# Dilated attention in a two-layer fp32 trunk: value products of two groups made wide, attention steps put in six places of a quarter, one group's scores in plain fp32

## The chip, the cores and the metric

The kernel runs on one core of one Trainium2 chip. The metric is the time of one execution on the device in microseconds, as the median of several runs. In the profile, PE is TensorE's matmul, PEld its weight load, DVE is VectorE, ACT is ScalarE, POOL is GpSimd and SP the engine that issues the loads. L12 is line 12 of the kernel's file.

## The reference

A trunk of two layers works on 256 tokens of width 1024, all in float32. Each layer is: half a SwiGLU feed-forward, a token mixer, half a second SwiGLU feed-forward, each behind an RMS norm and added to the residual. Layer 0 mixes with dilated window attention, layer 1 with latent attention. The change is in layer 0's mixer:

```python
A_PATTERNS = ((128, 1), (512, 4), (2048, 16))     # three groups of 16 heads of width 64
q, k, v = jnp.split(x @ w_in, 3, axis=-1)
q = rope(rmsnorm(q.reshape(shp), q_gain), pos)
k = rope(rmsnorm(k.reshape(shp), k_gain), pos)
for g, (window, dilation) in enumerate(A_PATTERNS):
    o, lse = _dilated_band(q[:, :, sl], k[:, :, sl], v[:, :, sl], window, dilation)
wts = jax.nn.softmax(jnp.stack(lses, axis=0), axis=0)
o = jnp.einsum('gbsh,gbshd->bshd', wts, jnp.stack(outs, axis=0))
return o.reshape(B, S, A_HEADS * A_HEAD_DIM) @ w_out
```

A token of group g attends to earlier tokens at distances that are multiples of the group's dilation, inside its window. The three groups' outputs of a head are merged with weights from their softmax denominators, which is the same as one softmax over the scores of all three groups.

## The kernel before

Every product of weights is taken in three terms: both sides are split into a high part, rounded to the reduced type fp32r, and a low part, and high x high, high x low and low x high are summed in PSUM. `piece` (L86 to L103) does it for the weights: SP loads 1 MB, ACT casts the high part (L101) and DVE subtracts it (L102), in four cuts in this layer. The normed activations stand transposed and split in `xh` and `xl`. Tokens are stored by their residue modulo 4, so that group 1 sees four blocks of 64 tokens, and group 2 sees them through a window that is shifted by 64 tokens.

The dilated layer goes through four quarters of four heads each (`hq`), and through the three groups in a quarter, which makes twelve units. A unit has:

- `qk_products`: q and k of four heads, 512 columns, for two token tiles; two weight pieces (halves of the model width), each 24 products of 512 columns (L483 to L485), with a `filler` between the halves. `norm_rope_a` (L654 to L674) then norms and rotates both token tiles on ACT, DVE and POOL.
- `v_products`: values of the four heads, 256 columns; one piece, 48 products of 256 columns (L499 to L501), then ACT's scaled copies into `v0` (group 0, L506) or `vc` (groups 1 and 2, L509, L512).
- a turn (`turn`, L520): eight PE transposes of the normed q and k; for group 0 ACT and DVE split the result into high and low parts (L526, L527), for the others ACT copies it (L529).

When a quarter's three units are done, its attention follows in six steps during the next quarter. Four of them take scores (`scores(i)`, two heads by one token tile): three fp32r terms for group 0 (L543, 256 keys), small fp32 products of 64x64 for groups 1 and 2 (L550), then the softmax on DVE and ACT (L394 to L401). One step later come the transposes of the weights p (L408, copied by ACT, L410), one more step later the products with the values (L574, L585). Step i thus holds scores(i), the transposes of i-1 and the outputs of i-2, in this order. The two heads of a step stand in rows 0 to 63 and 64 to 127 of PE.

`fill()` sets where this goes: it is called three times a unit (between the halves, behind the norm, behind the values), takes a turn if one waits, else the next attention step. So a quarter has nine places: three turns and six steps. The instructions of an engine run in one order, which a scheduler makes from the program's; it moves an instruction past others where it thinks that its inputs or its buffer are late. PSUM has four banks `acc` for the dense products, three banks `wk` for scores and all transposes, which are used in turn and come free when ACT or DVE has read them, and one bank `ob` for the outputs.

The last quarter's attention is put between parts of the output projection (`out_part`, 24 products of 256 columns for each pair of heads).

## Time and profile before

| | |
|---|---|
| time, median of 3 runs | 1155.69 us (1155.37 to 1155.75) |
| the profiled execution, its own time | 1156.32 us |
| its span | 1154.5 us |
| granted TensorE clock | 0.998 |
| dilated layer in it | 195.7 to 479.2 us, 283.5 us |
| PE busy in that stretch | 282.7 us |
| DVE, ACT busy in it | 224.9 us, 173.8 us |
| HBM read | 194.01 MB, 169 GB/s over the span |

The profile's page has the busy time of every engine, the chain of work that ended last, and groups of instructions. A row of the time line is start, length, engine, line, operation, out<-in and count; the length of a matmul there is its way through the array and overlaps with the next one's. A row of the chain of waits is start, length and what the chain ran through; its lengths do not overlap. An fp32 product is two records in the trace, an fp32r product and a transpose are one.

### The profile page before, as it was taken

The page shows a single profiled execution, that of the slowest core. Times are in us where ns is not written, and L with a number is a line of the kernel's source. Part 1 is how long each engine was busy: PE and PEld are TensorE (multiplying, and loading weights), DVE is VectorE, ACT ScalarE, POOL GpSimd, SP SyncE. Part 2 cuts the span into 40 slices and gives each one's busy share as a digit, 9 for nine tenths or more (in the row PEclk, how much of TensorE's full clock was granted, in tenths as well). Part 3 has the DMA queues.
Part 4 walks back from the last instruction along what each step waited for, and adds up shares of the span by engine and source line. Part 5 has one row for each costly group of instructions (what it writes and reads, how often), then busy time and mean ns, then how long its engine had stood idle before and what let it go on. Part 6 is the DMA issues. An engine that isn't in the chain of part 4 may idle for free.

```text
span 1154.5 us, 19404 instructions
## 1 busy us (share of the span) xinstructions
PE 1140.5 (99%) x7836; PEld 1026.4 (89%) x7836; DVE 836.8 (72%) x1469; ACT 642.8 (56%) x1090; POOL 106.1 (9%) x99
## 2 busy tenths in 40 slices
PE   9999999999999999999999999999999899999998
PEld 8999999888888888889999989999998788999997
DVE  6966667979788767776666796666687897666665
ACT  7544446566656565654544464444576776545442
POOL 2000002212112111200000020000023202000000
PEclk9999999999999999999999999999999999999999
DMA  8655554554443444255555545555532334555540
GB/s 324 233 200 182 183 186 143 219 183 147 146 151 142 145 148 147 93 200 183 192 194 196 180 173 196 183 183 188 193 110 104 110 127 177 181 191 195 189 146 37
DMA packets 29033, 196.30 MB, mean 170 GB/s; under 512 B 3344, under 2 KB 3856, under 8 KB 5904
## 3 DMA queue, kind: packets, MB, share of 16 engines
q1 hardware_dynamic: 28656, 194.55, 47.9%
q8 instruction: 61, 1.00, 0.4%
q10 hardware_dynamic: 288, 0.52, 0.2%
q14 instruction: 28, 0.23, 0.1%
HBM read 194.01 MB, written 1.05 MB: 169 GB/s over the span
## 4 chain that ended last, share of the span: by engine, by line
PE 92%; DVE 5%; ACT 2%; POOL 1%; issue 1%; DMA 0%; SPq 0%; DVEq 0%; POOLq 0%; ACTq 0%
PE up L210 27%; PE up L214 14%; PE acc L112 9%; PE acc L113 9%; PE acc L114 9%; PE acc L483 4%; PE acc L485 3%; PE acc L484 3%; PE acc L499 2%; PE acc L501 2%; PE acc L500 2%; DVE lo L102 2%; PE wk L408 2%; DVE xs L128 1%; PE wk L520 1%; PE ob L574 1%
## 5 line engine op out<-in xcount | busy, mean ns | idle before, releaser
L102 DVE TENSOR_TENSOR lo<-raw,hi 128x512 fp32r<-128x512 f32 (+2 forms) x408 | 448.5, 1124 | 231.8 <-ACT hi L101 231.4
L101 ACT CAST hi<-raw 128x512 fp32r<-128x512 f32 (+2 forms) x408 | 375.7, 964 | 215.8 <-issue 109.9
L210 PE MATMUL up<-xs,hi 128*128 128x512 f32 x1408 | 483.4, 396 | 1.2 <-ACT hi L101 0.7
L214 PE MATMUL up<-xs,lo 128*128 128x256 f32 x1408 | 366.0, 280 | 0.0
L210 PEld LDWEIGHTS up<-xs,hi 128*128 128x128 f32 x1408 | 252.4, 188 | 45.8 <-DVE xs L128 1.3
L214 PEld LDWEIGHTS up<-xs,lo 128*128 128x128 f32 x1408 | 266.3, 189 | 16.6 <-DVE lo L102 0.7
L113 PE MATMUL acc<-hl,hi 128*128 128x256 f32 x704 | 198.0, 282 | 0.2
L114 PE MATMUL acc<-hh,lo 128*128 128x256 f32 x704 | 197.6, 282 | 0.0
L112 PE MATMUL acc<-hh,hi 128*128 128x256 f32 x704 | 195.9, 281 | 0.2 <-ACT hh L237 0.2
L113 PEld LDWEIGHTS acc<-hl,hi 128*128 128x128 f32 x704 | 132.5, 188 | 1.1 <-DVE hl L238 1.0
L112 PEld LDWEIGHTS acc<-hh,hi 128*128 128x128 f32 x704 | 131.7, 188 | 1.8 <-ACT hh L237 0.6
L114 PEld LDWEIGHTS acc<-hh,lo 128*128 128x128 f32 x704 | 132.5, 188 | 0.0
L237 ACT CAST hh<-h 128x256 fp32r<-128x256 f32 x88 | 35.6, 406 | 142.8 <-DVE h L234 142.8
L483 PE MATMUL acc<-hi,xs 128*128 128x512 f32 x192 | 76.6, 399 | 0.0
L485 PE MATMUL acc<-hi,xs 128*128 128x512 f32 x192 | 75.2, 392 | 0.0
L484 PE MATMUL acc<-lo,xs 128*128 128x512 f32 x192 | 74.9, 390 | 0.0
L226 DVE TENSOR_TENSOR gu<-up,rest 128x512 f32<-128x512 f32 x88 | 60.1, 683 | 2.6 <-ACT rest L224 2.4
L230 DVE TENSOR_TENSOR gu<-gu,bc 128x512 f32<-128x512 f32 x88 | 60.2, 687 | 1.4
L143 POOL TENSOR_TENSOR ssq<-sq 128x256 f32<-128x256 f32 x6 | 4.9, 813 | 587.9 <-ACT sq L140 415.2
L659 POOL TENSOR_TENSOR rr<-r,mhalf 128x8 f32<-128x8 f32 x24 | 39.2, 1636 | 196.5 <-DVE r L657 196.5
L499 PE MATMUL acc<-hi,xs 128*128 128x256 f32 x192 | 55.3, 288 | 0.0
L501 PE MATMUL acc<-hi,xs 128*128 128x256 f32 x192 | 54.6, 284 | 0.0
(198 smaller groups left out, 1493.4 us busy)
## 6 DMA issues: line engine op xcount, KB each, us to landing
raw<-in_up SPq DMA_DIRECT2D x87, 1024.0 KB, 4.8
raw<-in_down SPq DMA_DIRECT2D x44, 1024.0 KB, 4.8
raw<-in_a_qk SPq DMA_DIRECT2D x24, 1024.0 KB, 4.8
raw<-in_a_v SPq DMA_DIRECT2D x12, 1024.0 KB, 4.8
raw<-in_a_out SPq DMA_DIRECT2D x4, 1024.0 KB, 4.7
raw<-in_b_out SPq DMA_DIRECT2D x4, 1024.0 KB, 5.0
raw<-in_b_in SPq DMA_DIRECT2D x3, 1024.0 KB, 4.8
raw<-in_b_q SPq DMA_DIRECT2D x4, 576.0 KB, 4.0
```

Of the source, the lines that this page charges most:

```text
L101: self.pin(pinned, nc.scalar.copy(hi[:, c], raw[:, c]))
L102: self.pin(pinned, nc.vector.tensor_tensor(lo[:, c], raw[:, c], hi.bitcast(F32)[:, c], op=ALU.subtract))
L112: self.nc.tensor.matmul(out, wh, xh, start=start and i == 0, stop=False, **kw)
L113: self.nc.tensor.matmul(out, wh, xl, start=False, stop=False, **kw)
L114: self.nc.tensor.matmul(out, wl, xh, start=False, stop=stop and i == n - 1, **kw)
L210: nc.tensor.matmul(ps[:, u].rearrange("p t s -> p (t s)"), hv[:, k, u, :], both, start=k == 0, stop=False, skip_group_check=True)
L214: nc.tensor.matmul(ps[:, u, 0, :], lv[:, k, u, :], xh[:, k, :], start=False, stop=k == KT - 1, skip_group_check=True)
L483: nc.tensor.matmul(pss[tt], xh, hi[:, k, :], start=kk == 0, stop=False)
L484: nc.tensor.matmul(pss[tt], xh, lo[:, k, :], start=False, stop=False)
L485: nc.tensor.matmul(pss[tt], xl, hi[:, k, :], start=False, stop=kk == KT - 1)
L499: nc.tensor.matmul(o, xh, hi[:, k, :], start=k == 0, stop=False)
L501: nc.tensor.matmul(o, xl, hi[:, k, :], start=False, stop=k == KT - 1)
```

## The change

Values of groups 0 and 1 are taken together: `v_near` runs two pieces like `qk_products`, two token tiles of 512 columns (24 products a half), and `v_far` takes group 2 alone, now with ACT's copies behind each of its two token windows instead of behind both. The weights are laid out to match; the number of pieces and of bytes is unchanged. Group 0's turned q and k are kept as plain fp32, and its scores are one fp32 product a head (now L536) in place of three terms. A step does its transposes first, then its outputs, then its scores. The places of a quarter are written out: the middle of q/k unit 0 (third turn and step 5 of the quarter before), behind the wide values (first turn, step 0), the middle of unit 1 (step 1), behind it (step 2), behind the far values (step 3), the middle of unit 2 (step 4, second turn). In the changed file L510 to L512 are all dense products (before L483 to L485 and L499 to L501), L543 are the small scores products (before L550), L567 and L578 the outputs (before L574 and L585); L520 and L408 keep their numbers.

```diff
-            def fill():
-                if turns:
-                    turns.pop(0)()
-                elif todo:
-                    todo.pop(0)()
-
...
+            low, up = slice(0, H), slice(H, P)
+
+            def v_near(hq, v0, vc, filler):
+
+                pss = [self.acc.tile([P, 512], F32, name="acc") for _ in range(NTT)]
+                for h in range(2):
+                    wp = [t.rearrange("p (k c) -> p k c", k=4) for t in self.piece(v_w[3 * hq + h], 4)]
+                    for tt in range(NTT):
+                        token_product(pss[tt], slice(tt * P, (tt + 1) * P), wp, 4 * h, 4)
+                    if h == 0:
+                        filler()
+                for tt in range(NTT):
+                    rs = self.rstd[:, tt : tt + 1]
+                    nc.scalar.activation(v0[:, tt, :], pss[tt][:, :S], AF.Copy, scale=rs)
+                    for a, rows in enumerate((low, up)):
+                        nc.scalar.activation(vc[rows, tt * 2 + a, :], pss[tt][rows, S:], AF.Copy, scale=rs[rows])
+
+            def v_far(hq, vc):
+
+                wp = [t.rearrange("p (k c) -> p k c", k=KT) for t in self.piece(v_w[3 * hq + 2], 4)]
                 ps = self.acc.tile([P, 512], F32, name="acc")
-                for tt in range(NTT):
-                    o = ps[:, tt * S : (tt + 1) * S]
-                    for k in range(KT):
-                        first = tt * P + (H if g == 2 else 0)
-                        xh, xl = (t[:, k, first : first + P] for t in (self.xh, self.xl))
-                        nc.tensor.matmul(o, xh, hi[:, k, :], start=k == 0, stop=False)
-                        nc.tensor.matmul(o, xh, lo[:, k, :], start=False, stop=False)
-                        nc.tensor.matmul(o, xl, hi[:, k, :], start=False, stop=k == KT - 1)
-                low, up = slice(0, H), slice(H, P)
-                for tt in range(NTT):
-                    o = ps[:, tt * S : (tt + 1) * S]
-                    if g == 0:
-                        nc.scalar.activation(v0[:, tt, :], o, AF.Copy, scale=self.rstd[:, tt : tt + 1])
-                    elif g == 1:
-                        for a, rows in enumerate((low, up)):
-                            nc.scalar.activation(vc[rows, tt * 2 + a, :], o[rows], AF.Copy, scale=self.rstd[rows, tt : tt + 1])
-                    else:
-                        for c, rows in ((tt * 2 + 1, low), ((1 - tt) * 2, up)):
-                            nc.scalar.activation(vc[rows, c, :], o[rows], AF.Copy, scale=rw[rows, tt : tt + 1])
+                for w in range(NTT):
+                    o = ps[:, w * S : (w + 1) * S]
+                    token_product(o, slice(w * P + H, (w + 1) * P + H), wp, 0, KT)
+                    for c, rows in ((w * 2 + 1, low), ((1 - w) * 2, up)):
+                        nc.scalar.activation(vc[rows, c, :], o[rows], AF.Copy, scale=rw[rows, w : w + 1])
+
+            def token_product(out, ts, wp, first, n):
+
+                hi, lo = wp
+                for k in range(n):
+                    kk = first + k
+                    xh, xl = self.xh[:, kk, ts], self.xl[:, kk, ts]
+                    nc.tensor.matmul(out, xh, hi[:, k, :], start=kk == 0, stop=False)
+                    nc.tensor.matmul(out, xh, lo[:, k, :], start=False, stop=False)
+                    nc.tensor.matmul(out, xl, hi[:, k, :], start=False, stop=kk == KT - 1)
 
...
-                    if isinstance(dst, tuple):
-                        hi, lo = dst
-                        nc.scalar.copy(hi, tpv)
-                        nc.vector.tensor_tensor(lo, tpv, hi.bitcast(F32), op=ALU.subtract)
-                    else:
-                        nc.scalar.copy(dst, tpv)
+                    nc.scalar.copy(dst, tpv)
 
...
-                    (qh, ql), (kh, kl) = qt[0], kt[0]
-                    for t, (a, b) in enumerate(((qh, kh), (qh, kl), (ql, kh))):
-                        for r in range(2):
-                            nc.tensor.matmul(ss[r][:, :S], a[rs[r], j, ts], b[rs[r], j, :], start=t == 0, stop=t == 2)
+                    for r in range(2):
+                        nc.tensor.matmul(ss[r][:, :S], qt[0][rs[r], j, ts], kt[0][rs[r], j, :], start=True, stop=True)
...
                 def step(i):
                     def go():
-                        if i < 4:
-                            scores(i)
                         if 0 <= i - 1 < 4:
                             turned(i - 1)
                         if 0 <= i - 2 < 4:
                             outputs(i - 2)
+                        if i < 4:
+                            scores(i)
 
                     return go
 
                 return [step(i) for i in range(6)]
 
+
+            steps, late = [lambda: None] * 6, []
             for hq in range(4):
-
-                qt, kt = (
-                    [tuple(at.tile([P, 2, S], F32R, name=n + x, bufs=2) for x in "hl")]
-                    + [at.tile([P, 2, S], F32, name=n, bufs=4) for _ in range(GA - 1)]
-                    for n in ("qt", "kt")
-                )
+                qt, kt = ([at.tile([P, 2, S], F32, name=n, bufs=6) for _ in range(GA)] for n in ("qt", "kt"))
                 v0 = at.tile([P, NTT, S], F32, name="v0", bufs=2)
                 vc = at.tile([P, 2 * NTT, S], F32, name="vc", bufs=2)
-                for g in range(GA):
-                    u = hq * GA + g
-                    if u < 4 * GA - 1:
-                        pss = qk_products(u, fill)
-                        if u == 0:
-                            self.stats()
-                            window_stats()
-                            nc.vector.tensor_scalar(ee, self.var, EPS, None, op0=ALU.mult)
-                        qkn = [self.norm_rope_a(at, pss[tt], tt, ee) for tt in range(NTT)]
-                        fill()
-                        v_products(u, g, v0, vc)
-                        fill()
-                    else:
-                        v_products(u, g, v0, vc)
-                        fill()
-                        pss = qk_products(u, fill)
-                        qkn = [self.norm_rope_a(at, pss[tt], tt, ee) for tt in range(NTT)]
-                        while todo:
-                            fill()
-                    turns.append(lambda qkn=qkn, d=(qt[g], kt[g]): turn(qkn, d))
-                todo.extend(attention(hq, qt, kt, v0, vc))
+
+                def qk(g, *midway):
+                    pss = qk_products(hq * GA + g, lambda: [f() for f in midway])
+                    if hq == 0 and g == 0:
+                        self.stats()
+                        window_stats()
+                        nc.vector.tensor_scalar(ee, self.var, EPS, None, op0=ALU.mult)
+                    qkn = [self.norm_rope_a(at, pss[tt], tt, ee) for tt in range(NTT)]
+                    return lambda d=(qt[g], kt[g]): turn(qkn, d)
+
+                turn0 = qk(0, *late)
+                v_near(hq, v0, vc, lambda: None)
+                turn0()
+                steps[0]()
+                turn1 = qk(1, steps[1])
+                steps[2]()
+                v_far(hq, vc)
+                steps[3]()
+                turn2 = qk(2, steps[4], turn1)
+                late = [turn2, steps[5]]
+                steps = attention(hq, qt, kt, v0, vc)
             out_part(0)
             out_part(1)
-            fill()
+            for f in late:
+                f()
             for k in range(2, KT - 2):
-                fill()
+                steps[k - 2]()
                 out_part(k, range(4 if k == KT - 3 else KT))
-            while todo:
-                fill()
+            steps[4]()
+            steps[5]()
             ks = range(KT - 3, KT)
             self.closing([(0, ks[1:]), (2, ks[1:]), (4, ks), (6, ks)], out_part, accs, finish, 1.0)
```

How the instructions stand on PE is shown at four places of the second quarter. First, where the first scores of a quarter stand. Before, in a place of their own between a unit's q/k and value products (kth, ktl, qth, qtl are the split parts of group 0):

```order
L485 MATMUL acc<-hi,xs 128x512
L543 MATMUL wk<-kth,qth 128x256 x2
L543 MATMUL wk<-ktl,qth 128x256 x2
L543 MATMUL wk<-kth,qtl 128x256 x2
L550 MATMUL wk<-kt,qt 64x64 x8
L499 MATMUL acc<-hi,xs 128x256
```

In the change, behind the last two of the first turn's eight transposes:

```order
L520 MATMUL wk<-ident,t_2660 128x128
L520 MATMUL wk<-ident,t_2674 128x128
L536 MATMUL wk<-kt,qt 128x256
L543 MATMUL wk<-kt,qt 64x64 x4
L510 MATMUL acc<-hi,xs 128x512
L536 MATMUL wk<-kt,qt 128x256
L543 MATMUL wk<-kt,qt 64x64 x4
L511 MATMUL acc<-lo,xs 128x512
```

The two heads, which stood together (x2), now stand apart, with one dense product between them.

Second, the step that ends the scores of a quarter, behind the last value products. Before:

```order
L501 MATMUL acc<-hi,xs 128x256
L543 MATMUL wk<-kth,qth 128x256 x2
L543 MATMUL wk<-ktl,qth 128x256 x2
L543 MATMUL wk<-kth,qtl 128x256 x2
L550 MATMUL wk<-kt,qt 64x64 x8
L408 MATMUL wk<-ident,p 128x128 x3
L574 MATMUL ob<-pt,v_2070 64x128 x3
L408 MATMUL wk<-ident,p 128x128 x3
L574 MATMUL ob<-pt,v_2070 64x128
L585 MATMUL ob<-pt,vc 64x64 x4
```

In the change:

```order
L512 MATMUL acc<-hi,xs 128x256
L408 MATMUL wk<-ident,p 128x128 x6
L536 MATMUL wk<-kt,qt 128x256
L543 MATMUL wk<-kt,qt 64x64 x2
L536 MATMUL wk<-kt,qt 128x256
L543 MATMUL wk<-kt,qt 64x64 x6
L512 MATMUL acc<-hi,xs 128x512
```

The six transposes are together; the outputs of this step have moved ahead, into the far values; and the second head's product stands behind two of the first head's small ones.

Third, where those outputs went, between the two token windows of the far values:

```order
L512 MATMUL acc<-hi,xs 128x256
L567 MATMUL ob<-pt,v_2068 64x128 x4
L578 MATMUL ob<-pt,vc 64x64 x4
L510 MATMUL acc<-hi,xs 128x512
L511 MATMUL acc<-lo,xs 128x512
L510 MATMUL acc<-hi,xs 128x256
```

The second window's first product (the last row) waits for ACT, which copies the first window's values out of the same bank; two products of the next unit stand ahead of it.

Fourth, the third turn and step 5, in the middle of the next quarter's first unit (t_3221 and t_3235 are the two token tiles). Before, turn and outputs had a place each, uncut; in the change:

```order
L512 MATMUL acc<-hi,xs 128x512
L520 MATMUL wk<-ident,t_3221 128x128 x2
L567 MATMUL ob<-pt,v_2068 64x128 x3
L520 MATMUL wk<-ident,t_3235 128x128
L520 MATMUL wk<-ident,t_3221 128x128
L520 MATMUL wk<-ident,t_3235 128x128 x2
L520 MATMUL wk<-ident,t_3221 128x128
L520 MATMUL wk<-ident,t_3235 128x128
L567 MATMUL ob<-pt,v_2068 64x128
L578 MATMUL ob<-pt,vc 64x64 x4
L510 MATMUL acc<-hi,xs 128x512
```

The outputs are split around six of the eight transposes. Other places hold their step in one piece: the second step is six transposes and the scores of both heads, the third six transposes, outputs and scores, the fifth six transposes, outputs and the second turn's eight transposes. Outside the dilated layer the order of every engine is as before.

More of the change, by code (lines that the diff above doesn't have):

```diff
@@ L452, in dilated @@
             out_part, accs = self.out_product(w_out, oth, otl)
-            todo, turns = [], []
             for t in (self.xh, self.xl):
@@ L476, in qk_products @@
                 for h in range(2):
-                    hi, lo = (t.rearrange("p (k c) -> p k c", k=4) for t in self.piece(qk_w[u, h], 4))
+                    wp = [t.rearrange("p (k c) -> p k c", k=4) for t in self.piece(qk_w[u, h], 4)]
                     for tt in range(NTT):
-                        for k in range(4):
-                            kk = h * 4 + k
-                            ts = slice(tt * P, (tt + 1) * P)
-                            xh, xl = self.xh[:, kk, ts], self.xl[:, kk, ts]
-                            nc.tensor.matmul(pss[tt], xh, hi[:, k, :], start=kk == 0, stop=False)
-                            nc.tensor.matmul(pss[tt], xh, lo[:, k, :], start=False, stop=False)
-                            nc.tensor.matmul(pss[tt], xl, hi[:, k, :], start=False, stop=kk == KT - 1)
+                        token_product(pss[tt], slice(tt * P, (tt + 1) * P), wp, 4 * h, 4)
                     if h == 0:
@@ new lines, in dilated @@
+            low, up = slice(0, H), slice(H, P)
[4 more added lines that the diff above has]
+                    for tt in range(NTT):
+                        token_product(pss[tt], slice(tt * P, (tt + 1) * P), wp, 4 * h, 4)
+                    if h == 0:
[5 more added lines that the diff above has]
+                        nc.scalar.activation(vc[rows, tt * 2 + a, :], pss[tt][rows, S:], AF.Copy, scale=rs[rows])
@@ L1024, in _layout @@
     a["a_qk"] = c(qk.reshape(4 * GA, 2, P, PIECE))
-    a["a_v"] = c(w[:, :, 2].transpose(3, 2, 1, 0, 4).reshape(4 * GA, P, PIECE))
+    v = w[:, :, 2].transpose(3, 1, 0, 2, 4)
+    near = v[:, :, :, :2].reshape(4, P, 2, PIECE).transpose(0, 2, 1, 3)
+    a["a_v"] = c(np.concatenate([near, v[:, None, :, :, 2].reshape(4, 1, P, PIECE)], axis=1).reshape(4 * GA, P, PIECE))
     a["a_out"] = c(i["a_w_out"][0].reshape(4, 2, P, D).transpose(0, 2, 1, 3).reshape(4, P, PIECE))
```

2 lines of the change are left out of this document (removed).

## The prediction

> **What bounds the kernel now.** I read the page's busy times and its chain of waits first, then the table of stretches for the dilated layer (195.7 to 479.2 us) and for two of its quarters, cut at the first scores product of a quarter.
>
> ```profile
> PE 1140.5 (99%) x7836; PEld 1026.4 (89%) x7836; DVE 836.8 (72%) x1469; ACT 642.8 (56%) x1090; POOL 106.1 (9%) x99
> PE 92%; DVE 5%; ACT 2%; POOL 1%; issue 1%; DMA 0%; SPq 0%; DVEq 0%; POOLq 0%; ACTq 0%
> ```
> ```profile
> 195.70:479.20 283.50, 282.70 (x2157) 246.10 (x2156) 224.94 (x489) 173.84 (x368) 47.81 (x34) 1.00 0.43 149
> 261.40:325.90 64.50, 64.50 (x491) 55.32 (x490) 51.48 (x115) 40.66 (x85) 9.81 (x7) 1.00 0.44 149
> 325.90:390.50 64.60, 64.60 (x491) 55.39 (x490) 51.58 (x115) 39.37 (x84) 9.86 (x7) 1.00 0.42 147
> ```
> The columns are length, then busy time of PE, PEld, DVE, ACT and POOL, the granted clock, the DMA share and GB/s. In a quarter PE is busy for all of its 64.5 us at full clock, DVE for 51.5 and ACT for 40.7. No wait is left to be taken away: a quarter gets shorter only if PE gets less to do, and any wait that comes new is paid in full. So I price PE's own work, by the distance between starts, since a busy time includes each product's way through the array.
>
> **The dense products.** From the chain of waits inside one stretch:
>
> ```profile
> 216.13 0.23 PE acc L484
> ...
> 219.76 0.23 PE acc L485
> ...
> 226.32 0.12 PE acc L499
> ...
> 232.07 0.23 PE acc L483
> ```
> Sixteen wide (512) products lie between the first two rows: 3.63/16 = 0.227 us. Forty-eight narrow (256) ones lie between the last two: 5.75/48 = 0.120 us. The change replaces eight blocks of 48 narrow products by four of 48 wide ones: 384 x 0.120 = 46.0 us become 192 x 0.227 = 43.5 us. That is **-2.5 us**, the one sure gain. The skill prices this otherwise: the Trainium skill, "TensorEngine Tiling (Array Packing)", section Instruction Overhead, gives each matmul about 60 cycles, which at the 2.4 GHz of its first page would make 192 fewer products worth an estimated 4.8 us; the two paces above allow 2 x 0.120 - 0.227 = 0.013 us a product, and I go by them.
>
> **The places between them.** I price a place as the distance from the last dense product before it to the second one after it, less two dense paces. A turn, a scores step, and a step of six transposes and outputs (PE's time line):
>
> ```profile
> 219.60 0.39 PE L485 MATMUL acc<-hi,xs 128*128 128x512 f32 x1
> 219.83 1.04 PE L520 MATMUL wk<-ident,t 128*128 128x128 f32 x8
> ...
> 220.93 0.40 PE L484 MATMUL acc<-lo,xs 128*128 128x512 f32 x1
> ```
> ```profile
> 325.56 0.39 PE L485 MATMUL acc<-hi,xs 128*128 128x512 f32 x1
> 325.88 0.39 PE L543 MATMUL wk<-kth,qth 64*128 64x256 f32 x2
> 326.11 0.28 PE L543 MATMUL wk<-ktl,qth 64*128 64x256 f32 x2
> 326.22 0.28 PE L543 MATMUL wk<-kth,qtl 64*128 64x256 f32 x2
> 326.43 0.46 PE L550 MATMUL wk<-kt,qt 64*64 64x64 f32 x16
> ...
> 327.05 0.28 PE L500 MATMUL acc<-lo,xs 128*128 128x256 f32 x1
> ```
> ```profile
> 305.34 0.39 PE L485 MATMUL acc<-hi,xs 128*128 128x512 f32 x1
> 305.57 0.82 PE L408 MATMUL wk<-ident,p 128*128 128x128 f32 x6
> 306.32 0.66 PE L574 MATMUL ob<-pt,v 128*64 128x128 f32 x8
> ...
> 307.36 0.28 PE L500 MATMUL acc<-lo,xs 128*128 128x256 f32 x1
> ```
> Turn: 1.33 - 0.45 = 0.88 us. Scores: 1.49 - 0.35 = 1.14. Transposes and outputs: 2.02 - 0.35 = 1.67, of which the six transposes are 0.65 and the outputs 1.02. Uncut, a quarter would need 3 x 0.88 + 4 x 1.14 + 4 x 1.67 = 13.9 us. A quarter of 64.55 us (the mean of the two) with 144 wide products (32.7) and 144 narrow ones (17.25) leaves 14.6. So cutting costs **0.73 us a quarter today**, most of it in the fourth step:
>
> ```profile
> 290.36 0.28 PE L501 MATMUL acc<-hi,xs 128*128 128x256 f32 x1
> ...
> 291.51 0.55 PE L408 MATMUL wk<-ident,p 128*128 128x128 f32 x3
> 291.98 0.65 PE L574 MATMUL ob<-pt,v 128*64 128x128 f32 x6
> 292.56 0.55 PE L408 MATMUL wk<-ident,p 128*128 128x128 f32 x3
> ...
> 293.97 0.39 PE L484 MATMUL acc<-lo,xs 128*128 128x512 f32 x1
> ```
> This place costs 3.61 - 0.35 = 3.26 where 1.14 + 1.67 = 2.81 would do. It also shows the price of a change of tile shape: a transpose takes 0.11 us (0.88 for the turn's eight), so three need 0.33, and 0.47 pass before the outputs start. I take 0.14 for each change.
>
> **Scores in fp32.** Each fp32 product is two records in the trace:
>
> ```profile
> 939.39 0.43 PE wk L825 x2
> ```
> So 256 columns need 2 x 0.217 = 0.43 us. Today the three term rows stand as x2: the two heads (rows 0-63 and 64-127) run side by side, three passes of 0.12, with the first stretched to 0.23. If the fp32 heads pair in the same way, two passes of 0.22 replace 0.46 us and the step stays at **1.14**. Bounds: 1.0 if the step from the 64x128 to the 64x64 shape is free once both are fp32, and 1.57 if the heads run one after the other. I take 1.14, since the pairing is in today's rows. The Trainium skill, "TensorEngine Tiling (Array Packing)", section Key Properties, says that a change of tiling mode drains the engine; by it the lower bound falls away, by the bound alone the sum would be 2.7 us less.
>
> **The new order, place by place.** By the words of the change the steps stay whole; the instruction order above shows that the scheduler still cuts three of a quarter's six places.
> *Turn and first scores:* head 0 alone, one wide product, head 1 alone. The trace has one such cut, in the last quarter:
>
> ```profile
> 448.69 0.28 PE L114 MATMUL acc<-oth,lo 128*128 128x256 f32 x1
> 448.81 1.03 PE L520 MATMUL wk<-ident,t 128*128 128x128 f32 x8
> 449.77 0.38 PE L543 MATMUL wk<-kth,qth 64*128 64x256 f32 x1
> ...
> 450.79 0.27 PE L113 MATMUL acc<-otl,hi 128*128 128x256 f32 x1
> ...
> 452.15 0.28 PE L112 MATMUL acc<-oth,hi 128*128 128x256 f32 x1
> ```
> 2.10 + 1.36 - 4 x 0.12 = 2.98 where 0.88 + 1.14 = 2.02 would do: +0.96. A lone head needs 0.43 now and 3 x 0.12 = 0.36 then, so **+1.1**.
> *Fourth step:* the second head's product stands behind two of the first head's small ones: 0.43 more, one pair of small passes alone (0.11), three more changes of shape (0.42): **+0.96**.
> *Last step, mixed with the third turn:* two more changes of shape and one output product without its partner (0.21): **+0.5**.
> *Second step:* the scores come straight behind the transposes and need the bank of the first three. PE and ACT rows of the last step show when it is free:
>
> ```profile
> 469.65 0.82 PE L408 MATMUL wk<-ident,p 128*128 128x128 f32 x6
> ```
> ```profile
> 470.23 0.86 ACT L410 COPY pt<-wk 128x384 f32<-128x384 f32 x2 [1.28 <-PE wk L408]
> ```
> The third transpose starts at 469.87; the copy starts 0.36 later and takes about 0.5 with the signals. PE could start the second head after 0.33 + 0.14 and gets the bank after 0.87, while the first head covers some of it: **+0.3**.
> *Third and fifth places:* merged, so one return to the full array less each: -0.2 and -0.1.
> Together +2.56 a quarter, where today has +0.73.
>
> The sum: three quarters, 3 x (2.56 - 0.73) = +5.5; the first of them has no outputs to mix with its turn, -0.4; the last quarter loses its cut of 0.96 and the fragment of 0.45, and gains the mixed turn (0.4), the bank wait (0.3) and a tail with four more changes and two lone output products (about 0.9), so +0.2; the far window +0.2 in three quarters, +0.6; the values -2.5. **+3.4 us.**
>
> The far window's term: its second half starts only when ACT has copied the first half out of the bank.
>
> ```profile
> L512 ACT ACTIVATE vc<-acc,rw 64x256 f32<-64x256 f32 x16 | 7.5, 469 | 13.8 <-PE acc L501 13.6
> L398 ACT ACTIVATE p<-p,mx 128x384 f32<-128x384 f32 x32 | 19.6, 615 | 5.7 <-DVE mx L394 5.7
> ```
> Two copies and the 0.36 to reach ACT are 1.3 us; the outputs and two wide products that the order puts in between cover 1.4. With ACT free that is 0; behind one softmax exponential of the step before it is up to 0.6; I take 0.2. In the first quarter five wide products cover it. Group 0's eight subtractions leave DVE, and I cost that at nothing: PE hides them today, with 13 us of a quarter in which DVE is idle, and would only feel them if DVE became the bound. The loads keep their number, and the weights' splits run two pieces ahead of PE in the new order as in the old.
>
> What would be late next is the third turn, now one half product (24 x 0.227 = 5.4 us) behind its unit:
>
> ```profile
> 441.87 0.39 PE L485 MATMUL acc<-hi,xs 128*128 128x512 f32 x1
> ```
> ```profile
> 446.45 0.68 DVE L102 TENSOR_TENSOR lo<-raw,hi 128x512 fp32r<-128x512 f32 x1
> 447.06 0.68 DVE L674 TENSOR_TENSOR t<-t,rr 128x512 f32<-128x512 f32 x1
> ```
> The second token tile was ready at 447.74, 5.9 us after the unit's last product, with one split and one small subtraction ahead of it; now two splits stand there, 6.1. PE reaches its transposes after 5.4 + 0.2 + two transposes and three outputs (0.8) = 6.4. I cost it at nothing, with 0.3 us of cover.
>
> **The rivals.** *The cuts are free (faster).* If PE slips the second head in beside whatever runs, places cost their uncut sum: the quarter goes from +0.73 to -0.3, 3 x -1.03 = -3.1, the last quarter gives -1.1 (its tail stays whole), the far window +0.6 and the values -2.5: -6.1 us, 1149.6. Its place is the turn with the first scores. It decides once a quarter's cuts cost under 1.4 us in place of 2.56; near that the time is unchanged. For it: heads do pair where they stand together. Against it: at 449.77 and 451.00 the heads did not. *The fp32 heads do not pair:* ten steps keep both heads together, 10 x 0.43 = +4.3, so 1163.4. Today's fp32r pairs speak against it. *The third turn is late:* each split that DVE still has to do when the unit ends adds 0.6 us; three in each of three quarters, less the cover, are +4.5, 1163.6. DVE's load (51.5 of 64.5) allows it. *The overhead rule:* -2.3 more, 1156.8, against both paces.
>
> **How the numbers follow.** The profiled execution took 1156.3 us (span 1154.5), 0.6 above the median 1155.7. With +3.4 it would be 1159.7, and the median **1159.1**. Forecast 0.58, by its bounds (shape changes free -2.7; waits +2.5) 1156.4 to 1161.6; cuts free or half free 0.20; heads unpaired 0.08; late turn 0.12; overhead rule 0.02. A measurement of this kernel tells 0.2% (2.3 us) from no change. Faster: 0.09, from the free cuts. Same: 0.11 from half-free cuts, 0.14 from the low end of the forecast, 0.02 from the overhead rule, 0.27. Slower: 0.64. Range 1155.0 to 1164.5.
>
> **What would show it.** Right: no PE idle time, a steady quarter of about 65.7 us, the turn with first scores near 3.1, where two L536 rows follow each other, both heads' records starting within 0.01 us and the second pass 0.22 later. Wrong: a quarter under 64.5; L536 heads 0.43 apart where they stand together; PE waiting for DVE at L520.

## The result and the profile after

The changed kernel takes 1163.39 us (median of 4 runs, 1162.25 to 1164.46) where the kernel before, on the same chip, takes 1155.72. The ratio is 1.0060, with a 95% interval of 1.0044 to 1.0076. So it is slower, by about 7 us. The forecast was 1159.1: right in its sign and inside its range, but half of the size.

The profiled execution took 1162.64 us, with a span of 1160.9. Busy times and the chain of waits from the page of the changed kernel:

```profile
PE 1145.0 (99%) x7612; PEld 1018.2 (88%) x7612; DVE 832.0 (72%) x1461; ACT 643.3 (55%) x1090; POOL 105.0 (9%) x99
PE 91%; DVE 5%; ACT 2%; DMA 1%; POOL 1%; issue 1%; SPq 0%; DVEq 0%; POOLq 0%; ACTq 0%
```

PE has 224 products fewer and is busy 4.5 us longer. Where that lies is seen in stretches. The columns are as in the prediction: length, then busy time of PE, PEld, DVE, ACT and POOL. First the kernel before, from its first dense product of the layer to the last one of its last unit, and from there to the end of the layer; then the same two stretches of the changed kernel, and one steady quarter of it:

```profile
195.68:441.87 246.19, 245.39 (x1763) 212.01 (x1762) 198.57 (x423) 152.60 (x317) 42.05 (x30) 1.00 0.45 157
441.87:479.17 37.30, 37.30 (x394) 34.08 (x393) 26.36 (x67) 21.23 (x51) 5.76 (x5) 1.00 0.29 100
```
```profile
195.65:446.89 251.24, 250.57 (x1548) 205.10 (x1547) 192.99 (x415) 152.29 (x317) 42.02 (x30) 1.00 0.43 153
446.89:484.85 37.96, 37.94 (x386) 33.70 (x385) 26.29 (x66) 22.13 (x51) 4.98 (x5) 1.00 0.27 97
272.64:339.18 66.54, 66.54 (x433) 54.00 (x432) 50.19 (x112) 40.61 (x86) 9.81 (x6) 1.00 0.41 143
```

The dilated layer grew from 283.49 to 289.20 us, by 5.71: 5.05 in the quarters and 0.66 in the tail. Behind the layer another 0.6 is lost: PE's wait where the feed-forward starts grew by 1.0, and the rest took 0.4 less. PE's waits around that point, before and after (line waited at, who released it, us, times, longest):

```profile
PE up L210 <- DVE xs L128: 0.2, 1, 0.2
```
```profile
PE up L210 <- DVE xs L128: 1.2, 1, 1.2
```

A steady quarter takes 66.5 us where it took 64.5. The price of a place is taken as in the prediction: the distance from the last dense product ahead of it to the second one behind it, less two dense paces. The turn with the first scores (PE's time line of the changed kernel):

```profile
271.67 1.03 PE L520 MATMUL wk<-ident,t 128*128 128x128 f32 x8
272.64 0.70 PE L536 MATMUL wk<-kt,qt 64*128 64x256 f32 x2
273.26 0.45 PE L543 MATMUL wk<-kt,qt 64*64 64x64 f32 x8
273.64 0.49 PE L510 MATMUL acc<-hi,xs 128*128 128x512 f32 x1
274.06 0.70 PE L536 MATMUL wk<-kt,qt 64*128 64x256 f32 x2
274.69 0.45 PE L543 MATMUL wk<-kt,qt 64*64 64x64 f32 x8
275.07 0.50 PE L511 MATMUL acc<-lo,xs 128*128 128x512 f32 x1
```

Each head alone needs 0.62 us for its two fp32 records (272.64 to 273.26) and 0.38 for its small products. The second place, on PE and on ACT:

```profile
280.42 0.82 PE L408 MATMUL wk<-ident,p 128*128 128x128 f32 x6
281.17 1.24 PE L536 MATMUL wk<-kt,qt 64*128 64x256 f32 x4
282.34 0.46 PE L543 MATMUL wk<-kt,qt 64*64 64x64 f32 x16
282.73 0.50 PE L510 MATMUL acc<-hi,xs 128*128 128x512 f32 x1
```
```profile
280.67 0.62 ACT L101 CAST hi<-raw 128x512 fp32r<-128x512 f32 x1 [1.57 <-issue]
281.19 0.85 ACT L410 COPY pt<-wk 128x384 f32<-128x384 f32 x2
```

The four fp32 records stand in one row, but 1.17 us pass from the first to the small products: the heads ran one behind the other, since the second one's bank is free only after the first of the two copies (it ends at 281.66, and the second head starts at 281.72, 0.54 behind the first). That copy stands behind a weight cast on ACT and starts 0.55 us after the third transpose (280.64, two paces of 0.11 behind the first). The fourth place:

```profile
298.23 0.82 PE L408 MATMUL wk<-ident,p 128*128 128x128 f32 x6
298.98 0.70 PE L536 MATMUL wk<-kt,qt 64*128 64x256 f32 x2
299.60 0.33 PE L543 MATMUL wk<-kt,qt 64*64 64x64 f32 x4
299.94 0.70 PE L536 MATMUL wk<-kt,qt 64*128 64x256 f32 x2
300.56 0.45 PE L543 MATMUL wk<-kt,qt 64*64 64x64 f32 x12
300.94 0.50 PE L512 MATMUL acc<-hi,xs 128*128 128x512 f32 x1
```
```profile
298.43 0.95 ACT L502 ACTIVATE vc<-acc,rw 64x256 f32<-64x256 f32 x2 [3.01 <-PE acc L512]
299.40 0.86 ACT L410 COPY pt<-wk 128x384 f32<-128x384 f32 x2
```

Here ACT copies the far values first, and the first of the transposes only from 299.40 on; PE starts the second head at 299.94. All places of a steady quarter, before and after, with the uncut price that the prediction used:

| place | uncut, by the prediction | forecast | measured |
|---|---|---|---|
| turn and first scores | 2.02 | +1.1 | 3.29 (+1.27) |
| second: transposes, scores | 1.79 | +0.3 | 2.42 (+0.63) |
| third: transposes, outputs, scores | 2.81 | -0.2 | 2.70 (-0.11) |
| outputs between the far windows | 1.02 | +0.2 | 1.01 (0.0) |
| fourth: transposes, scores | 1.79 | +0.96 | 2.82 (+1.03) |
| fifth: transposes, outputs, turn | 2.55 | -0.1 | 2.51 (-0.04) |
| third turn with step 5 | 1.90 | +0.5 | 2.40 (+0.50) |

### The profile page after: what moved, and what is told of

Read it like the earlier page. It is cut to its first block, busy times and chain, and to the rows that moved or that the text cites. A ratio compares the mean times of both kernels' runs of the same rounds, so it can differ in the third digit from the quotient of the medians.

```text
span 1160.9 us, 18978 instructions
## 1 busy us (share of the span) xinstructions
PE 1145.0 (99%) x7612; PEld 1018.2 (88%) x7612; DVE 832.0 (72%) x1461; ACT 643.3 (55%) x1090; POOL 105.0 (9%) x99
## 4 chain that ended last, share of the span: by engine, by line
PE 91%; DVE 5%; ACT 2%; DMA 1%; POOL 1%; issue 1%; SPq 0%; DVEq 0%; POOLq 0%; ACTq 0%
PE up L210 26%; PE up L214 14%; PE acc L113 9%; PE acc L112 9%; PE acc L114 8%; PE acc L510 6%; PE acc L512 5%; PE acc L511 5%; DVE lo L102 2%; PE wk L408 1%; PE wk L536 1%; DVE xs L128 1%; PE wk L520 1%; DMA raw<-in_up 1%; PE ob L567 1%; PE wk L543 1%
## 5 line engine op out<-in xcount | busy, mean ns | idle before, releaser
L510 PE MATMUL acc<-hi,xs 128*128 128x512 f32 (+1 forms) x320 | 120.2, 376 | 0.0
L512 PE MATMUL acc<-hi,xs 128*128 128x512 f32 (+1 forms) x320 | 118.2, 370 | 0.0
L511 PE MATMUL acc<-lo,xs 128*128 128x512 f32 (+1 forms) x320 | 118.1, 370 | 0.0
L510 PEld LDWEIGHTS acc<-hi,xs 128*128 128x128 f32 x320 | 60.3, 188 | 10.6 <-ACT vc L502 0.4
L512 PEld LDWEIGHTS acc<-hi,xs 128*128 128x128 f32 x320 | 60.2, 188 | 10.0
L511 PEld LDWEIGHTS acc<-lo,xs 128*128 128x128 f32 x320 | 60.3, 188 | 9.7
```

What stands on the lines that cost most here:

```text
L510: nc.tensor.matmul(out, xh, hi[:, k, :], start=kk == 0, stop=False)
L511: nc.tensor.matmul(out, xh, lo[:, k, :], start=False, stop=False)
L512: nc.tensor.matmul(out, xl, hi[:, k, :], start=False, stop=kk == KT - 1)
```

## The experiments

The time of a whole execution varies by some 4 us: the kernel before took 1155.8 to 1159.6 us on one chip. The last section shows what most of that is. The dilated layer's own length in a profile, from its first dense product to the first product behind it, varies less (the steady quarters of a profile agree to 0.02 us), so each run is read by both. The length is from one profile each, at a granted clock of 1.00 in the layer but for the one marked row. The ratio is to the kernel before on the same chip.

| kernel | ratio, 95% interval | dilated layer, us | against before |
|---|---|---|---|
| before | | 283.49 | |
| changed | 1.0060 (1.0044 to 1.0076) | 289.20 | +5.71 |
| wide values alone | 0.9976 (0.9967 to 0.9985) | 280.54 | -2.95 |
| fp32 scores alone | 1.0024 (1.0015 to 1.0033) | 286.05 | +2.56 |
| new order alone | 1.0066 (1.0053 to 1.0080) | 290.58 | +7.09 |
| changed, far copies behind | 1.0047 (1.0033 to 1.0061) | 288.78 | +5.29 |
| the same, uncut | 1.0094 (1.0070 to 1.0119) | 288.71 | +5.22 |
| uncut, free bank | 1.0020 (1.0012 to 1.0029) | 280.27 | -3.22 |
| uncut, free bank, fp32r | 1.0004 (0.9996 to 1.0013) | 281.01 (3.4 us of it at half the clock) | -2.48 |
| changed, fp32r | 1.0047 (1.0035 to 1.0059) | 288.45 | +4.96 |
| far copies behind, free bank | 0.9983 (0.9973 to 0.9993) | 280.41 | -3.08 |
| the same, fp32r, outputs ahead of the third turn | 0.9956 (0.9942 to 0.9969) | 278.51 | -4.98 |
| free bank, first scores apart | 1.0014 (1.0005 to 1.0022) | 283.92 | +0.43 |
| free bank, outputs ahead of the third turn | 0.9968 (0.9958 to 0.9978) | 279.27 | -4.22 |

### The three parts, each alone

Wide values in the kernel before, with its nine places:

```diff
-                        v_products(u, g, v0, vc)
-                        fill()
+                    if g == 0:
+                        v_near(hq, v0, vc, fill)
+                    elif g == 1:
+                        v_far(hq, vc)
...
+                    if g < 2:
+                        fill()
```


> The kernel before with one part of the change alone: values of groups 0 and 1 wide, of group 2 narrow with the copies behind each window; nine places a quarter, steps and scores as before. Theory (PE's prices): 192 fewer products, -2.5 us, and the wait between the far windows, measured in the changed kernel as 1.23 against 1.02 us for the outputs there, at most +0.8 over four quarters: 1153.2 to 1154.0. Rival A (wide values are the loss, by late norms or late copies): no faster than 1155.7. Rival B (the cuts that the scheduler makes new in this order eat it): 1155 to 1157.

Measured: 2.95 us less in the layer, 0.24% less time. A steady quarter takes 63.73 us where it took 64.55. Of the 0.8 less, 0.6 is the dense term, 0.013 us for each of 48 products, and 0.2 lies in the places between; over the layer that is the 2.5 of the prediction and about 0.5. The layer is 0.4 us better than the theory. That separates the two prices of the prediction. Read as time that each product adds, the cycles of the Trainium skill, "TensorEngine Tiling (Array Packing)", section Instruction Overhead, would have made it an estimated 4.8; the measurement decides for 2.5.

Group 0's scores in fp32, in the kernel before:

```diff
-                    (qh, ql), (kh, kl) = qt[0], kt[0]
-                    for t, (a, b) in enumerate(((qh, kh), (qh, kl), (ql, kh))):
-                        for r in range(2):
-                            nc.tensor.matmul(ss[r][:, :S], a[rs[r], j, ts], b[rs[r], j, :], start=t == 0, stop=t == 2)
+                    for r in range(2):
+                        nc.tensor.matmul(ss[r][:, :S], qt[0][rs[r], j, ts], kt[0][rs[r], j, :], start=True, stop=True)
```


> The kernel before with group 0's scores as one fp32 product a head and its turned q and k kept plain; nothing else. Theory: the heads pair, but the step is longer by what the changed kernel's third place shows, 0.63 us from the first fp32 record to the first small product where the three fp32r terms took 0.55: 16 x 0.08 = +1.3, so 1157.0. Rival A (the price in my prediction, fp32 costs nothing): 1155.7. Rival B (heads one after the other where they stand together): +0.4 a step and more, above 1161.

The heads pair: their two records each fill one 0.70 us row, and 0.64 us separate it from the small products (PE's time line):

```profile
325.89 0.39 PE L485 MATMUL acc<-hi,xs 128*128 128x512 f32 x1
326.20 0.70 PE L536 MATMUL wk<-kt,qt 64*128 64x256 f32 x4
326.84 0.46 PE L543 MATMUL wk<-kt,qt 64*64 64x64 f32 x16
```

The place costs 1.22 us where it cost 1.14: 16 x 0.08 = 1.3 of the 2.56. The theory had that and missed the rest, 1.3 us. A steady quarter takes 65.08 us where it took 64.55: 0.32 of that is its four steps, and most of the other 0.2 lies in three transposes that the old order cuts off behind the second step, 0.62 us where they cost 0.41. Three quarters give 0.7 beyond the steps. The other 0.6 comes in the last quarter, most of it in one step that the scheduler cuts in another way there (3.40 us where it cost 2.82, with 0.19 in which PE waits for DVE). Why the cuts fall otherwise is open. Both rivals fall.

The new order alone, with narrow values and three fp32r terms (against the changed kernel; the scores and the split turns go back as above):

```diff
-                v_near(hq, v0, vc, lambda: None)
+                v_products(hq * GA, 0, v0, vc)
+                v_products(hq * GA + 1, 1, v0, vc)
...
-                v_far(hq, vc)
+                v_products(hq * GA + 2, 2, v0, vc)
```


> The kernel before with the new places and the new order in a step alone: narrow values, scores in three fp32r terms. Theory (the three parts add): the changed kernel's +7 without -2.5 for the wide values, +1.3 for fp32 and +0.8 for the far window is +7.4, so 1163.1. Rival A (order costs only my predicted 1.8 a quarter, about +5.6): 1161.3. Rival B (the loss needs the parts together, and the order alone is harmless): under 1158.

It loses 7.09 us by itself: the theory's 7.4, and neither rival. So the loss is in the places and in the order inside a step, and the wide values take 3 us of it back. The three parts sum to +6.7 where the change has +5.7; they don't add exactly.

The fp32 scores taken back from the changed kernel:

> The changed kernel with one part undone: group 0's scores in three fp32r terms. Theory: 16 x 0.08 = 1.3 less than the changed kernel, stretch 287.9 for 289.2, about +5.5 us over the kernel before. Rival A (in the kernel before fp32 alone cost 2.6 in the stretch): 286.6. Rival B (where PE waits for banks, the shorter scores only wait longer): 289.2, no change.

The layer is 0.75 us shorter, between the theory (1.3) and rival B. In the new order fp32 is a small part of the loss.

### The copies of the far values

```diff
                 for w in range(NTT):
-                    o = ps[:, w * S : (w + 1) * S]
-                    token_product(o, slice(w * P + H, (w + 1) * P + H), wp, 0, KT)
+                    token_product(ps[:, w * S : (w + 1) * S], slice(w * P + H, (w + 1) * P + H), wp, 0, KT)
+                for w in range(NTT):
+                    o = ps[:, w * S : (w + 1) * S]
                     for c, rows in ((w * 2 + 1, low), ((1 - w) * 2, up)):
```


> The changed kernel with ACT's copies of the far values behind both windows again, so that the second window has nothing to wait for. Theory: the place between the windows took 1.23 us where outputs alone take 1.02; 4 x 0.2 = 0.8 less than the changed kernel, so about +6.2 us over the kernel before. Rival A: the wait is hidden or comes back at another place, no change against the changed kernel (+7). Rival B: the later copies delay the step that waits for the values, more than +7.5.

The layer is 0.42 us shorter where the theory had 0.8; 0.3 of that lies in the first quarter, and 0.05 in a steady one. The intervals of the two times overlap. The 1.23 us in the expectation counted the two wide products behind the outputs as narrow ones: the place between the windows costs 1.01 in the changed kernel, the price of the outputs alone. In a steady quarter the second window waits for nothing there.

### Cut, or late bank

In the second place the heads stand together and still ran one behind the other. So the question is whether cutting the steps costs, or the bank that comes late. First, PE was held to the program's order in steps and turns:

```diff
+            keep = tc.keep_in_program_order
...
-                            nc.tensor.transpose(
+                            keep(nc.tensor.transpose(
...
-                        nc.tensor.matmul(ss[r][:, :S], qt[0][rs[r], j, ts], kt[0][rs[r], j, :], start=True, stop=True)
+                        keep(nc.tensor.matmul(ss[r][:, :S], qt[0][rs[r], j, ts], kt[0][rs[r], j, :], start=True, stop=True))
```


> The changed kernel with the far values' copies behind both windows, and PE held to the program's order in the steps and turns, so that no step is cut: each place is whole, both heads follow each other. The third bank that a step needs still has to be copied out by ACT first. Theory (a cut costs by the heads that run alone, and a bank that comes late costs too): turn with first scores 3.29 to 2.65 us, third turn with step 5 2.41 to 1.87, the places that wait for a bank (second, fourth) unchanged: -1.2 in three quarters, so the dilated stretch goes from 288.8 (far copies behind alone) to 285.2, about +2 us over the kernel before. Rival A (the cuts alone are the loss, and PE's own work is all that is left): every place at its uncut price, 3 x -2.9 = -8.7, stretch about 280. Rival B (the cuts are the scheduler's good answer to the late bank, and PE stands still instead): 288.8 or more.

The layer takes 288.71 us, as long as with the cuts (288.78): rival B. PE's time line at the turn with the first scores, and at the third turn:

```profile
339.37 1.03 PE L525 MATMUL wk<-ident,t 128*128 128x128 f32 x8
340.33 0.70 PE L541 MATMUL wk<-kt,qt 64*128 64x256 f32 x2
341.54 0.70 PE L541 MATMUL wk<-kt,qt 64*128 64x256 f32 x2 [0.51 <-ACT qt L529]
342.17 0.46 PE L548 MATMUL wk<-kt,qt 64*64 64x64 f32 x16
342.56 0.50 PE L511 MATMUL acc<-hi,xs 128*128 128x512 f32 x1
...
387.14 0.27 PE L525 MATMUL wk<-ident,t 128*128 128x128 f32 x1
387.67 0.99 PE L525 MATMUL wk<-ident,t 128*128 128x128 f32 x7 [0.26 <-DVE t L670]
```

The first head ends and PE stands still for 0.51 us until ACT has copied the first half of the turn out of the bank; the place costs 3.30 us, as much as cut (3.29). The small products of the first head stand ready behind the second head's product and aren't taken first. The Trainium skill, "TensorE: Matmul & The Clock Gate", Part 3, section The mechanism, says that products start and end strictly in order and only weight loads are pulled ahead; this trace agrees. At the third turn PE waits from 387.25, when the second transpose was due, to 387.67: 0.42 us for DVE's second token tile; 2.38 us uncut, 2.40 cut. There too the cut was the scheduler's filling of a wait.

Then the cause was taken away: the second head of steps 0, 1 and 3 gets one of the four banks of the dense products, so that none of the three banks of the transposes is waited for.

```diff
-                    ss = [self.wk.tile([P, 512], F32, name="wk") for _ in range(2)]
+                    ss = [self.wk.tile([P, 512], F32, name="wk")]
+                    third = hq < 3 and i in (0, 1, 3)
+                    ss.append(self.acc.tile([P, 512], F32, name="acc") if third else self.wk.tile([P, 512], F32, name="wk"))
```


> As the uncut kernel, but the second head's scores of steps 0, 1 and 3 go into one of the four banks of the dense products instead of the three that the transposes use too, so that no score waits for a copy of transposes. Theory (the late bank is the second half of the loss): -0.55 at the turn with first scores, -0.55 at the second place, -0.9 at the fourth: 3 x -2.0 = -6.0 against the uncut kernel, stretch about 279, 4 us under the kernel before. Rival A (heads would be apart anyway, the bank isn't what is waited for): no change against the uncut kernel. Rival B (the dense products then wait for their banks): slower than the uncut kernel.

288.71 becomes 280.27: 8.4 us less, more than the theory's 6.0; both rivals fall. The places are 2.10 (from 3.30), 1.88 (from 2.42), 2.70 (from 3.79 for the fourth place with its outputs): 2.8 us a quarter. The time fell less against the kernel before than the layer did (ratio 1.0020): the uncut kernels have another order in the latent layer too, and the program behind the dilated layer, from its first product to its last, took 675.9 us where it took 671.2. A part of that is one more stretch at half the clock, of the kind in the last section; the uncut kernel without the free bank, which has only one such stretch, as the kernel before has, took 674.4. Uncut kernels are therefore compared with each other, and the same step was made with the scheduler's own order, which leaves the rest of the program as it was:

> The changed kernel with the far values' copies behind both windows and the second head's scores of steps 0, 1 and 3 in a bank of the dense products; PE's order is left to the scheduler, and the latent layer stands as in the kernel before. Theory (late banks are the loss): the stretch of the dilated layer goes from 288.8 (far copies behind alone, +5.4 us in time) to about 280.3, so 8 us less: 2.5 to 3 us under the kernel before. Rival (the gain in the uncut pair came from the uncut order, and holds only there): 285 to 288 in the stretch, above the kernel before.

280.41 in the layer, 8.4 under the kernel with late banks, and 0.17% under the kernel before in time (2 us; the theory had 2.5 to 3). The gain doesn't need the uncut order: with a free bank the scheduler leaves the heads together. PE's time line at the turn with the first scores (wk and acc are the banks of the two heads):

```profile
335.63 1.04 PE L521 MATMUL wk<-ident,t 128*128 128x128 f32 x8
336.59 0.48 PE L539 MATMUL wk<-kt,qt 64*128 64x256 f32 x1
336.60 0.48 PE L539 MATMUL acc<-kt,qt 64*128 64x256 f32 x1
336.91 0.38 PE L539 MATMUL wk<-kt,qt 64*128 64x256 f32 x1
...
337.23 0.27 PE L546 MATMUL wk<-kt,qt 64*64 64x64 f32 x1
```

The heads start 0.01 us apart, and the second pass comes 0.32 behind the first.

Last, whether a cut costs where no bank is late. Only the first scores were put apart again, one wide product between the heads:

```diff
+                    if i == 0 and hq < 3:
+                        ps[i] = p_of
+                        head(0)
+                        apart.append(lambda: head(1))
+                        return
...
                     nc.tensor.matmul(out, xh, hi[:, k, :], start=kk == 0, stop=False)
+                    while apart:
+                        apart.pop()()
```


> The kernel with the free bank, and in the place of the turn with first scores alone the two heads apart by one wide product, as the scheduler had them in the changed kernel, though no bank is late now. Theory A (my prediction's price: heads that stand apart cost by themselves): that place goes from 2.10 to about 3.3 us, so the stretch from 280.4 to 284.0, +2.1 us over the kernel before. Theory B (only the late bank costs, and PE overlaps the parts): place near 2.1, stretch 280.4.

```profile
337.72 0.70 PE L545 MATMUL wk<-kt,qt 64*128 64x256 f32 x2
338.35 0.45 PE L550 MATMUL wk<-kt,qt 64*64 64x64 f32 x8
338.73 0.49 PE L513 MATMUL acc<-hi,xs 128*128 128x512 f32 x1
339.15 0.70 PE L545 MATMUL acc<-kt,qt 64*128 64x256 f32 x2
339.78 0.45 PE L550 MATMUL acc<-kt,qt 64*64 64x64 f32 x8
```

283.92: theory A, to 0.1 us. Heads that stand apart cost 1.17 us a place by themselves, 3.5 over three quarters, with nothing to wait for. The second head alone is 1.0 of it (339.15 to 340.16); the other 0.2 lies at the changes between dense and score products. So the cut and the late bank cost the same at this place, and either one is enough: the price in the prediction was right, but taking the cut away gains nothing while the bank is late.

### A kernel that beats both

The free bank with three fp32r terms, held to the program's order:

> As the uncut kernel with the free bank, and group 0's scores in three fp32r terms again. Theory: an fp32 pass in 64 rows by 256 takes 0.31 us where two stand for three terms of 0.12 to 0.23, 0.08 a step: 16 x 0.08 = -1.3 against the kernel with fp32, stretch about 277.7, 5.8 us under the kernel before. Rival: with everything hidden, DVE and ACT (24 us of splits come back over the layer) become what PE waits for, no gain or a loss.

Against the uncut kernel with the free bank, a quarter's places fell from 14.27 to 13.93 us, four times the 0.08 of the theory. The layer's 281.01 holds a stretch at half the clock (last section), about 1.6 us of it; the comparison of the layers is spoilt by that, and the one of the times has overlapping intervals. The rival isn't excluded by this run alone. Its 24 us of splits are too many: what comes back are eight subtractions on DVE, 5.5 us, while ACT's casts take the place of its copies.

Step 5 ahead of the third turn, so that the outputs cover DVE:

```diff
-                late = [turn2, steps[5]]
+                late = [steps[5], turn2]
```


> The kernel with the free bank, and step 5 ahead of the third turn in their place; fp32 scores as in the change. Theory (the turn waits 0.42 us for DVE's second token tile, which the outputs can cover): the place goes from 2.41 to 1.85, 3 x -0.56 = -1.7, stretch 278.7; then fp32r scores would have to be worth 0.2 of the best kernel's 278.5. Rival (the wait moves behind the outputs and fp32r is what the best kernel gained): 280.0 or more.

```profile
379.50 0.66 PE L570 MATMUL ob<-pt,v 128*64 128x128 f32 x8
379.99 0.40 PE L581 MATMUL ob<-pt,vc 128*64 128x64 f32 x8
380.32 1.09 PE L521 MATMUL wk<-ident,t 128*128 128x128 f32 x8
381.17 0.48 PE L511 MATMUL acc<-hi,xs 128*128 128x512 f32 x1
```

The place costs 1.85 us, no wait is left in it, and the layer falls by 1.14 to 279.27. The theory had 1.7 for three such places. There are two: in the first quarter no outputs wait yet, and in the tail the old order was kept. 2 x 0.56 is 1.1. With fp32r terms besides:

> As the kernel with the free bank, with group 0's scores in three fp32r terms again, and step 5 ahead of the third turn in its place, so that the outputs cover what the turn waits for (0.42 us for the second token tile). Theory: 280.3 less 16 x 0.08 for the scores and 3 x 0.45 for the turn is 277.7: 5.7 us under the kernel before, 2.8 under the wide values alone. Rival A (the splits that come back load DVE, and the turn is later by them): 279.5 or more. Rival B (the dense products wait for the banks that scores now hold): 281 or more.

278.51 in the layer and 0.44% less time than the kernel before (5 us), where wide values alone give 0.24%. The forecast was 277.7; fp32r gave 0.76 over the kernel with fp32 in place of 1.3. Rivals A and B fall. The intervals of the two times just touch; what separates the two kernels is the layer, 278.51 against 280.54. With the free bank and fp32 scores the new order is only level with wide values alone (280.41), so what this kernel gains over them is the outputs ahead of the turn, 1.14, and fp32r, 0.76.

## Why the prediction was right in sign and half in size

The profiled pair moved by 6.3 us where the sum had 3.4. Going through its steps:

- **What bounds.** Right: PE is busy for the whole of a steady quarter, and every place is paid in full.
- **The dense products.** Right: -2.5.
- **Scores in fp32.** The step that failed most. The prediction priced the pair as two passes of 0.22, 0.44 us, against 0.46 for the three terms with their stretched first pass. The fp32 pair has the stretch too: 0.32 from the first pass to the second where the prediction had 0.22, and 0.64 to the small products (326.20 to 326.84) where the three terms take 0.55 (325.88 to 326.43). A step costs 1.22 in place of 1.14, four times a quarter: 0.33 of the 0.6 us that a steady quarter was under-priced by (it took 2.0 more; the terms gave 1.4, that is 66.0 us, and the 65.7 named as the check was itself 0.3 under them). The heads do pair, so that rival falls.
- **Turn with first scores.** The size holds (+1.27, forecast +1.1, and 0.08 of the difference is fp32). The price of the cut is right too, as the run with the heads apart shows. But it is not the only reason: the second head's bank is late, uncut the place costs the same, and with a free bank the scheduler doesn't cut.
- **Second place.** The mechanism was right, a bank that ACT must free, and its size was half: +0.63 for a forecast of +0.3, 0.08 of it fp32. The prediction let the first head cover part of the wait. In the trace the copy starts 0.55 us after the third transpose, behind a weight cast, not 0.36, and the second head runs alone behind the first.
- **Fourth place.** +1.03 for +0.96, a fit that is in part luck: only changes of shape and lone passes were counted, but ACT has the far values to copy first. Held uncut, this place with its outputs costs the same 3.79, and with a free bank 2.70. What the cut would cost by itself here was not measured.
- **Last step with the third turn.** +0.50, as forecast, but by luck, since the cause is another. It was costed as changes of shape and a lone output, and the late third turn at nothing with 0.3 us of cover. The turn is late by 0.42 us, and the cut fills that; outputs ahead of the turn bring it to 1.85.
- **The far window.** Forecast +0.6, measured close to 0 in steady quarters and 0.3 in the first.
- **Tail and what follows.** Forecast +0.2 for the last quarter, measured +0.66; 0.32 of that is four steps in fp32. The wait for the first split of the feed-forward, 1.2 for 0.2 us, was not in the sum. It comes with the new order: the kernel with the order alone has it (1.3), those with wide values or fp32 scores alone do not (0.2), the best kernel still has 1.2, and the uncut kernels have none. What makes DVE late there is open.

Three quarters, each under-priced by 0.6, are 1.8, the tail 0.5, the feed-forward 0.6: the 2.9 us that were missing. Of the rivals, free cuts are refuted by the run with the heads apart; the late turn happened, but smaller than its 4.5 us.

## What to carry to other kernels

When a scheduler cuts a step, look for the buffer or the input that it takes to be late, since holding the order only turns the cut into a wait; here one more bank for the second head was worth 8.4 us, and uncutting nothing. Two products that run side by side in two halves of PE's rows must stand together in its queue: with one other product between them the second is paid in full, 1.17 us here. A step that copies out of a bank just ahead of one that needs it wants other work between, or a bank from another pool.

## What the runs showed that was not expected

A change that holds the order in one layer moved the order of another: in the uncut kernels PE's instructions in the latent layer, which wasn't touched, stand differently, and the program behind the dilated layer took 674.4 to 675.9 us where it took 671.2. And PE's clock can be halved for a short stretch. The profile of the uncut kernel with the free bank and fp32r has one on its first values (PE's time line; then a stretch with the granted clock, third number from the end):

```profile
208.76 0.38 PE L461 MATMUL ob<-ones,ssq 128*128 128x1 f32 x2 [1.45 <-DVE var L167]
...
209.65 0.63 PE L514 MATMUL acc<-lo,xs 128*128 128x512 f32 x1
210.07 0.63 PE L515 MATMUL acc<-hi,xs 128*128 128x512 f32 x1
```
```profile
209.50:213.00 3.50, 3.50 (x9) 2.75 (x9) 2.35 (x8) 0.64 (x2) 3.50 (x4) 0.51 0.00 0
```

Wide products came 0.43 us apart in place of 0.227, eight of them, about 1.6 us, behind a wait of 1.45 us. The kernel with fp32 waited 1.50 us at the same point without it. It is the only such stretch inside a dilated layer, but not the only one: 12 of the 14 profiles have one of 3.4 us in the latent layer, starting within 2 us of the end of a wait of some 1.98 us. In the kernel before (PE's time line, and the stretch):

```profile
899.57 0.64 PE L813 MATMUL wk<-ident,qn 128*96 128x128 f32 x4 [1.98 <-ACT qt L816]
```
```profile
900.90:904.30 3.40, 3.40 (x12) 2.57 (x11) 2.61 (x17) 1.91 (x7) 1.01 (x1) 0.50 0.15 63
```

Four of the profiles have another behind a wait of 1.25 us there. The profile of the new order alone has the same waits and no such stretch. Executions of one kernel differ in this: on one chip the kernel before took 1155.8 to 1156.4 us where the granted clock was 0.998 to 1.000, and 1157.4 to 1158.4 where it was 0.996. That is most of the spread of the times. The Trainium skill, "TensorE: Matmul & The Clock Gate", section HAM oscillation — how this bites in real kernels, puts the rule at idle gaps of over some 3.4 us; by these traces a shorter one can be followed by a halved clock, and isn't always.
